# Layer normalisation bound by its transfers: hand-placed semaphores in one critical section, and the reciprocal moved to GpSimd as a power

## The chip, the core and the metric

The kernel runs on one core of one Trainium2 chip. The core has five engines that matter here: VectorE (DVE in the profile), ScalarE (ACT), GpSimd (POOL), SyncE (SP, which here only issues transfers) and 16 DMA engines that move data between the chip's main memory (HBM) and the core's working memory (SBUF). The metric is the device time of one execution in microseconds, the median of several. The profile's span runs from the first to the last instruction and is some 1.7 to 2.3 us shorter than the time.

## The reference, cut to what matters

```python
batch, seq, dim = 32, 512, 1024          # x: 64 MB of float32
def reference(x, eps):                   # eps = 1e-5
    mean = np.mean(x, axis=-1, keepdims=True)
    var = np.var(x, axis=-1, keepdims=True)
    return ((x - mean) / np.sqrt(var + eps)).astype(np.float32)
```

16,384 rows of 1,024 numbers are each normalised on their own. 67.1 MB have to be read and 67.1 MB written.

## The kernel before

SBUF holds a ring with places for 50 rows in each of 128 partitions. The work goes in 15 tiles of 2 to 10 rows per partition. A tile is loaded into its place, normalised there, and stored from there; then the place is free for a later tile. The framework (Tile) finds the dependencies and places the semaphores.

```python
TILES = (4, 6, 10, 10, 10, 10, 10, 10, 10, 10, 10, 10, 10, 6, 2)
RING = 50
GROUP = 10      # rows computed together
FINE = 6        # ... in the last LAST tiles
LAST = 3

def group(xs, G):
    # VectorE: two statistics per row: (count, mean, squared deviations) of each half of 512
    for k in range(G): ... nc.vector.bn_stats(out=stats[:, k, s, :], in_=xs[:, k, ...])
    # GpSimd: nine small operations that merge them into -mean (nmean) and the sum of squares (ss)
    ...
    nc.scalar.activation(out=std[:, :G], in_=ss[:, :G], func=AF.Sqrt, bias=eps_t, scale=1.0 / D)
    nc.vector.reciprocal(out=rstd[:, :G], in_=std[:, :G])
    nc.gpsimd.tensor_mul(out=nmr[:, :G], in0=nmean[:, :G], in1=rstd[:, :G])
    for k in range(G):     # ScalarE: x * rstd + nmr, in place
        nc.scalar.activation(out=xs[:, k, :], in_=xs[:, k, :], func=AF.Identity,
                             bias=nmr[:, k : k + 1], scale=rstd[:, k : k + 1])

with tc.manual_schedule():
    for t, (K, row, pos) in enumerate(plan):
        nc.sync.dma_start(out=ring[:, pos : pos + K, :], in_=rows_of(x2, row, K))      # load
        step = FINE if t >= len(TILES) - LAST else GROUP
        for g in range(0, K, step): ... group(...)
        nc.scalar.dma_start(out=rows_of(o2, row, K), in_=ring[:, pos : pos + K, :])    # store
```

I count tiles, loads and stores from 0: store 12 is the store of the last tile of 10 rows, third from the end.

## Time and profile before

| | before |
|---|---|
| time, median of the first 3 runs | 318.13 us (318.11 to 318.26) |
| span of the profiled run | 316.6 us |
| busy: VectorE, ScalarE, GpSimd | 49%, 48%, 12% |
| share of the DMA engines' time: loads, stores | 49.6%, 49.1% |
| mean rate | 424 GB/s |
| first load issued, its first packet | 0.72 us, 1.75 us |
| last packet ends, span ends | 315.2 us, 316.6 us |

The last two rows and some later numbers come from the trace's packet records, which give queue, size, start and duration of every packet that a DMA engine moved. The profile has no name for the engine of a packet, but each transfer is completed by all 16 of them one by one, and the time from the first to the last completion, called the *spread* below, says how far the engines have drifted apart.

Three lines of ScalarE's timeline (start, length, what; in brackets its idle time and what ended it) show the path of the first tile: the square root, four normalisations, and the issue of the first store.

```profile
16.10 0.30 ACT L95 ACTIVATE std<-ss,eps_t 128x4 f32<-128x4 f32 x1 [13.88 <-POOL ss L60]
16.92 4.63 ACT L103 ACTIVATE ring<-ring,nmr,rstd 128x1024 f32<-128x1024 f32 x4 [0.53 <-POOL nmr L101]
21.58 0.37 ACTq L127 DMA_DIRECT2D out_dram<-ring  x1
```

### The profile page before, as it was taken

To read this page: it belongs to the slowest core of one execution; us is meant where nothing else is said; L and a number is where in the kernel's file an instruction comes from. 1 tells how busy PE (TensorE), PEld (TensorE's weight loads), DVE (VectorE), ACT (ScalarE), POOL (GpSimd) and SP (SyncE) were. 2 spreads that over 40 slices of the span, in tenths; PEclk is the share of its full clock that TensorE was granted. 3 is DMA by queue.
4 is the path that set the end of the run, shared out by engine and by line. 5 is a ranking of instruction groups with operands and counts; after the bars stand their busy time and mean duration, and the time that the engine had idled before them with its cause. 6 is when DMAs were issued, how large, how long until landed. Compare 5 with 4: busy or idle time off the path is not lost.

```text
span 316.6 us, 712 instructions
## 1 busy us (share of the span) xinstructions
DVE 156.5 (49%) x273; ACT 152.6 (48%) x145; POOL 37.5 (12%) x164
## 2 busy tenths in 40 slices
DVE  0692939539139229229319309409509509654300
ACT  1065329294490391291292192193094094591730
POOL 0202030200300300300300300300300200222200
DMA  8999999999999999999999999999999999999995
GB/s 308 437 424 401 411 466 430 432 419 440 446 435 414 430 457 430 424 419 466 430 424 419 450 435 436 414 430 445 450 414 424 450 438 408 444 421 426 463 407 247
DMA packets 4324, 134.25 MB, mean 424 GB/s; under 512 B 480, under 2 KB 480, under 8 KB 480
## 3 DMA queue, kind: packets, MB, share of 16 engines
q1 hardware_dynamic: 2160, 67.11, 49.6%
q10 hardware_dynamic: 2160, 67.11, 49.1%
q14 instruction: 4, 0.03, 0.0%
HBM read 67.11 MB, written 67.11 MB: 424 GB/s over the span
## 4 chain that ended last, share of the span: by engine, by line
DMA 42%; DVE 26%; another core or an unknown queue 14%; POOL 6%; ACT 5%; issue 3%; SPq 0%; DVEq 0%; POOLq 0%
DMA ring<-in_x_dram 29%; DVE stats L68 26%; DMA out_dram<-ring 13%; ACT ring L103 4%; POOL half L57 1%; POOL dev L89 1%; ACT std L95 1%; POOL dev L92 1%; POOL dev L82 1%; POOL nmean L79 1%; POOL dev L88 1%; POOL nmean L60 1%; POOL ss L60 1%; DVE rstd L99 0%
## 5 line engine op out<-in xcount | busy, mean ns | idle before, releaser
L68 DVE BATCH_NORM_STATS2 stats<-ring 128x6 f32<-128x512 f32 x256 | 153.4, 677 | 92.5 <-DMA ring<-in_x_dram 92.5
L103 ACT ACTIVATE ring<-ring,nmr,rstd 128x1024 f32<-128x1024 f32 x128 | 146.5, 1226 | 8.9 <-POOL nmr L101 8.9
L95 ACT ACTIVATE std<-ss,eps_t 128x10 f32<-128x10 f32 (+3 forms) x16 | 4.8, 301 | 141.7 <-POOL ss L60 141.7
L57 POOL TENSOR_TENSOR half<-stats 128x20 f32<-128x20 f32 (+3 forms) x16 | 3.7, 233 | 243.2 <-DVE stats L68 243.2
L99 DVE RECIPROCAL rstd<-std 128x10 f32<-128x10 f32 (+3 forms) x16 | 3.3, 204 | 51.7 <-ACT std L95 51.7
L89 POOL TENSOR_SCALAR dev<-dev 128x40 f32<-128x40 f32 (+3 forms) x16 | 4.6, 289 | 1.4
L101 POOL TENSOR_TENSOR nmr<-nmean,rstd 128x10 f32<-128x10 f32 (+3 forms) x16 | 3.3, 205 | 10.4 <-DVE rstd L99 10.4
L92 POOL TENSOR_TENSOR dev<-dev,stats 128x40 f32<-128x40 f32 (+3 forms) x16 | 4.1, 259 | 1.3
L79 POOL TENSOR_SCALAR nmean<-nmean 128x10 f32<-128x10 f32 (+3 forms) x16 | 3.9, 244 | 1.4
L82 POOL TENSOR_TENSOR dev<-stats,nmean 128x40 f32<-128x40 f32 (+3 forms) x16 | 3.9, 245 | 1.3
L88 POOL TENSOR_TENSOR dev<-dev 128x40 f32<-128x40 f32 (+3 forms) x16 | 3.8, 239 | 1.3
L57 POOL TENSOR_TENSOR half<-dev 128x20 f32<-128x20 f32 (+3 forms) x16 | 3.4, 212 | 1.3
L60 POOL TENSOR_TENSOR nmean<-half 128x10 f32<-128x10 f32 (+3 forms) x16 | 3.2, 203 | 1.3
L60 POOL TENSOR_TENSOR ss<-half 128x10 f32<-128x10 f32 (+3 forms) x16 | 3.2, 203 | 1.3
L95 ACT ACT_TABLE_LOAD x1 | 1.3, 1283 | 0.9 <-DVE eps_t L120 0.9
L120 DVE MEMSET eps_t<- 128x1 f32 x1 | 0.1, 59 | 0.8 <-PEq L144 0.8
L144 POOL MEMSET const-float32-0.0<- 128x1 f32 x1 | 0.1, 98 | 0.2 <-issue 0.2
L144 POOL MEMSET const-uint8-127<- 128x1 uint8 x1 | 0.1, 102 | 0.0
L144 POOL MEMSET const-bfloat16-1.0<- 128x1 bf16 x1 | 0.1, 101 | 0.0
L144 POOL MEMSET const-float32-1.0<- 128x1 f32 x1 | 0.1, 98 | 0.0
## 6 DMA issues: line engine op xcount, KB each, us to landing
ring<-in_x_dram SPq DMA_DIRECT2D x11, 5120.0 KB, 52.4
out_dram<-ring ACTq DMA_DIRECT2D x11, 5120.0 KB, 41.0
ring<-in_x_dram SPq DMA_DIRECT2D x2, 3072.0 KB, 30.7
out_dram<-ring ACTq DMA_DIRECT2D x2, 3072.0 KB, 22.0
ring<-in_x_dram SPq DMA_DIRECT2D x1, 2048.0 KB, 7.8
out_dram<-ring ACTq DMA_DIRECT2D x1, 2048.0 KB, 22.4
ring<-in_x_dram SPq DMA_DIRECT2D x1, 1024.0 KB, 61.0
out_dram<-ring ACTq DMA_DIRECT2D x1, 1024.0 KB, 11.4
```

The lines of the kernel that those rows point to most:

```text
L57: nc.gpsimd.tensor_tensor(out=half[:, :G], in0=terms[:, :, 0:2], in1=terms[:, :, 2:4], op=ALU.add)
L60: nc.gpsimd.tensor_tensor(out=o, in0=half[:, :G, 0], in1=half[:, :G, 1], op=ALU.add)
L68: nc.vector.bn_stats(out=stats[:, k, s, :], in_=xs[:, k, s * BN_MAX : (s + 1) * BN_MAX],)
L79: nc.gpsimd.tensor_scalar(out=nmean[:, :G], in0=nmean[:, :G], scalar1=-1.0 / H, scalar2=None, op0=ALU.mult)
L82: nc.gpsimd.tensor_tensor(out=dev[:, :G], in0=mean4, in1=nmean[:, :G].unsqueeze(2).to_broadcast([P, G, H]), op=ALU.add,)
L88: nc.gpsimd.tensor_mul(out=dev[:, :G], in0=dev[:, :G], in1=dev[:, :G])
L89: nc.gpsimd.tensor_scalar(out=dev[:, :G], in0=dev[:, :G], scalar1=float(D // H), scalar2=None, op0=ALU.mult)
L92: nc.gpsimd.tensor_tensor(out=dev[:, :G], in0=dev[:, :G], in1=m2, op=ALU.add)
L95: nc.scalar.activation(out=std[:, :G], in_=ss[:, :G], func=AF.Sqrt, bias=eps_t, scale=1.0 / D)
L99: nc.vector.reciprocal(out=rstd[:, :G], in_=std[:, :G])
L101: nc.gpsimd.tensor_mul(out=nmr[:, :G], in0=nmean[:, :G], in1=rstd[:, :G])
L103: nc.scalar.activation(out=xs[:, k, :], in_=xs[:, k, :], func=AF.Identity, bias=nmr[:, k : k + 1], scale=rstd[:, k : k + 1],)
```

## The change

The intent: free VectorE from waiting for its reciprocal (51.7 us of waits), let it run ahead through all statistics, and replace the framework's semaphores by few hand-placed ones.

```diff
-RING = 50
-GROUP = 10
-FINE = 6
-LAST = 3
+SLOT, SLOTS = 10, 5
...
+    ctx.enter_context(tc.tile_critical(no_gpsimd_drain=True))
...
+    stored = {p: sem(f"stored_{p[0]}_{p[1]}") for p in places}     # one count of stores per ring place
+    taken, pool, act = sem("taken"), sem("pool"), sem("act")
...
-        nc.vector.reciprocal(out=rstd[:, :G], in_=std[:, :G])
+        n = gp(
+            g.tensor_tensor(
+                out=rstd[:, b, :K], in0=std[:, b, :K], in1=power[:, :K], op=ALU.pow    # power = -1
+            ),
+            other=(act, row + t + 1),
+        )
...
+    for p in places:
+        n = sum(1 for q in plan if (q[2], q[0]) == p)
+        nc.sync.wait_ge(stored[p], 16 * n)
```

(Cut: the same GpSimd operations and normalisations as before, each with its wait and its increment written out.) One thing goes without a word of its own: with `FINE` and `LAST` the splitting of the last 10-row tile into 6 + 4 rows for computing is gone.

More of the change, by code (lines that the diff above doesn't have):

```diff
@@ L10 @@
 TILES = (4, 6, 10, 10, 10, 10, 10, 10, 10, 10, 10, 10, 10, 6, 2)
-RING = 50
-GROUP = 10
-FINE = 6
-LAST = 3
+SLOT, SLOTS = 10, 5
+FIRST, TURNS = 3, 2
 @with_exitstack
@@ L38 @@
     assert sum(TILES) * P == N
-    rings = ctx.enter_context(tc.tile_pool(name="rings", bufs=1))
-    st = ctx.enter_context(tc.tile_pool(name="st", bufs=3))
-    sm = ctx.enter_context(tc.tile_pool(name="sm", bufs=10))
     fdt = mybir.dt.float32
@@ L46, with sbuf @@
     ALU = mybir.AluOpType
-    ring = rings.tile([P, RING, D], fdt)
-    eps_t = rings.tile([P, 1], fdt)
+    def sbuf(name, shape):
+        return ctx.enter_context(nc.sbuf_tensor(name, shape, fdt))
+    plan, row, pos = [], 0, 0
+    for K in TILES:
+        at = pos % (SLOT * SLOTS)
+        plan.append((K, row, at, at // SLOT))
+        row += K
+        pos += K
+    ctx.enter_context(tc.tile_critical(no_gpsimd_drain=True))
+    ring = sbuf("ring", [P, SLOT * SLOTS, D])
+    stats = sbuf("stats", [P, SLOT * SLOTS, NSUB, 6])
@@ new lines @@
+    half = sbuf("half", [P, SLOT, 2])
+    dev = sbuf("dev", [P, SLOT, H])
+    ss, nmean, std, rstd, nmr = (
+        sbuf(n, [P, 2, SLOT]) for n in ("ss", "nmean", "std", "rstd", "nmr")
+    )
+    eps_t = sbuf("eps_t", [P, 1])
+    power = sbuf("power", [P, SLOT])
+    sem = nc.alloc_semaphore
+    places = sorted({(at, K) for K, row, at, slot in plan})
+    landed = [sem(f"landed_{t}") for t in range(FIRST + SLOTS)]
+    for t in range(len(landed), len(plan)):
+        looped = t < FIRST + TURNS * SLOTS
+        landed.append(landed[t - SLOTS] if looped else sem(f"landed_{t}"))
@@ L51, in rows_of @@
+    stored = {p: sem(f"stored_{p[0]}_{p[1]}") for p in places}
+    taken, pool, act = sem("taken"), sem("pool"), sem("act")
     def rows_of(a, row, K):
         return a[row * P : (row + K) * P].rearrange("(p k) d -> p k d", p=P)
-    def pool_sum(o, terms):
-        G = terms.shape[1]
-        half = sm.tile([P, GROUP, 2], fdt, name="half")
-        nc.gpsimd.tensor_tensor(
-            out=half[:, :G], in0=terms[:, :, 0:2], in1=terms[:, :, 2:4], op=ALU.add
-        )
-        nc.gpsimd.tensor_tensor(
-            out=o, in0=half[:, :G, 0], in1=half[:, :G, 1], op=ALU.add
-        )
@@ L64, in group @@
-    def group(xs, G):
-        stats = st.tile([P, GROUP, NSUB, 6], fdt, name="stats")
-        for k in range(G):
-            for s in range(NSUB):
-                nc.vector.bn_stats(
-                    out=stats[:, k, s, :],
-                    in_=xs[:, k, s * BN_MAX : (s + 1) * BN_MAX],
-                )
-        parts = stats[:, :G].rearrange("p g s (h c) -> p g (s h) c", h=2)
-        mean4, m2 = parts[:, :, :, 1], parts[:, :, :, 2]
-        nmean = sm.tile([P, GROUP], fdt, name="nmean")
-        dev = sm.tile([P, GROUP, H], fdt, name="dev")
-        ss = sm.tile([P, GROUP], fdt, name="ss")
-        pool_sum(nmean[:, :G], mean4)
-        nc.gpsimd.tensor_scalar(
-            out=nmean[:, :G], in0=nmean[:, :G], scalar1=-1.0 / H, scalar2=None, op0=ALU.mult
-        )
-        nc.gpsimd.tensor_tensor(
-            out=dev[:, :G],
-            in0=mean4,
-            in1=nmean[:, :G].unsqueeze(2).to_broadcast([P, G, H]),
-            op=ALU.add,
-        )
-        nc.gpsimd.tensor_mul(out=dev[:, :G], in0=dev[:, :G], in1=dev[:, :G])
-        nc.gpsimd.tensor_scalar(
-            out=dev[:, :G], in0=dev[:, :G], scalar1=float(D // H), scalar2=None, op0=ALU.mult
-        )
-        nc.gpsimd.tensor_tensor(out=dev[:, :G], in0=dev[:, :G], in1=m2, op=ALU.add)
-        pool_sum(ss[:, :G], dev[:, :G])
-        std = sm.tile([P, GROUP], fdt, name="std")
-        nc.scalar.activation(
-            out=std[:, :G], in_=ss[:, :G], func=AF.Sqrt, bias=eps_t, scale=1.0 / D
-        )
-        rstd = sm.tile([P, GROUP], fdt, name="rstd")
-        nc.vector.reciprocal(out=rstd[:, :G], in_=std[:, :G])
-        nmr = sm.tile([P, GROUP], fdt, name="nmr")
-        nc.gpsimd.tensor_mul(out=nmr[:, :G], in0=nmean[:, :G], in1=rstd[:, :G])
-        for k in range(G):
-            nc.scalar.activation(
-                out=xs[:, k, :],
-                in_=xs[:, k, :],
-                func=AF.Identity,
-                bias=nmr[:, k : k + 1],
-                scale=rstd[:, k : k + 1],
-            )
@@ L111 @@
-    plan, row, pos = [], 0, 0
-    for K in TILES:
-        if pos + K > RING:
-            pos = 0
-        plan.append((K, row, pos))
-        row += K
-        pos += K
-    with tc.manual_schedule():
-        nc.vector.memset(eps_t, eps_val)
-        for t, (K, row, pos) in enumerate(plan):
-            nc.sync.dma_start(out=ring[:, pos : pos + K, :], in_=rows_of(x2, row, K))
-            step = FINE if t >= len(TILES) - LAST else GROUP
-            for g in range(0, K, step):
-                G = min(step, K - g)
-                group(ring[:, pos + g : pos + g + G, :], G)
-            nc.scalar.dma_start(out=rows_of(o2, row, K), in_=ring[:, pos : pos + K, :])
+    owner, wait = {}, []
@@ new lines @@
+    count = {p: 0 for p in places}
+    for t, (K, row, at, slot) in enumerate(plan):
+        gone = sorted({owner[r] for r in range(at, at + K) if r in owner})
+        for g in gone:
+            p = plan[g][2], plan[g][0]
+            if g == gone[-1]:
+                break
+            nc.sync.wait_ge(stored[p], 16 * sum(1 for q in plan[: g + 1] if (q[2], q[0]) == p))
+        dma = nc.sync.dma_start(out=ring[:, at : at + K, :], in_=rows_of(x2, row, K))
+        if gone:
+            p = plan[gone[-1]][2], plan[gone[-1]][0]
+            n = sum(1 for q in plan[: gone[-1] + 1] if (q[2], q[0]) == p)
+            dma._wait_ge(stored[p], 16 * n)
+        dma.then_inc(landed[t], 16)
+        owner.update((r, t) for r in range(at, at + K))
@@ new lines, in statistics @@
+    def statistics(t, arrived):
+        K, row, at, slot = plan[t]
+        for k in range(K):
+            for s in range(NSUB):
+                i = nc.vector.bn_stats(
+                    out=stats[:, at + k, s, :],
+                    in_=ring[:, at + k, s * BN_MAX : (s + 1) * BN_MAX],
+                )
+                if k == 0 and s == 0:
+                    i._wait_ge(landed[t], arrived)
+                if k == K - 1 and s == NSUB - 1:
+                    i.then_inc(taken, 1)
+    nc.vector.memset(eps_t[:], eps_val)
@@ new lines, with gp @@
+    nc.vector.memset(power[:], -1.0)
+    for t in range(len(plan)):
+        turn = (t - FIRST) // SLOTS if FIRST <= t < FIRST + TURNS * SLOTS else 0
+        statistics(t, 16 * (turn + 1))
+    npool, after_std, ready = 0, [], []
+    def gp(i, own=None, other=None):
+        nonlocal npool
+        if other is not None:
+            i._wait_ge(*other)
+        elif own:
+            i._wait_ge(pool, own)
+        i.then_inc(pool, 1)
+        npool += 1
+        return npool
+    g = nc.gpsimd
@@ new lines @@
+    for t, (K, row, at, slot) in enumerate(plan):
+        b = t % 2
+        parts = stats[:, at : at + K].rearrange("p g s (h c) -> p g (s h) c", h=2)
+        mean4, m2 = parts[:, :, :, 1], parts[:, :, :, 2]
+        nm, d, h = nmean[:, b, :K], dev[:, :K], half[:, :K]
+        n = gp(
+            g.tensor_tensor(out=h, in0=mean4[:, :, 0:2], in1=mean4[:, :, 2:4], op=ALU.add),
+            other=(taken, t + 1),
+        )
+        n = gp(g.tensor_tensor(out=nm, in0=h[:, :, 0], in1=h[:, :, 1], op=ALU.add), n)
+        n = gp(
+            g.tensor_scalar(out=nm, in0=nm, scalar1=-1.0 / H, scalar2=None, op0=ALU.mult), n
+        )
+        n = gp(
+            g.tensor_tensor(
+                out=d, in0=mean4, in1=nm.unsqueeze(2).to_broadcast([P, K, H]), op=ALU.add
+            ),
+            n,
+        )
+        n = gp(g.tensor_mul(out=d, in0=d, in1=d), n)
+        n = gp(
+            g.tensor_scalar(
+                out=d, in0=d, scalar1=float(D // H), scalar2=None, op0=ALU.mult
+            ),
+            n,
+        )
+        n = gp(g.tensor_tensor(out=d, in0=d, in1=m2, op=ALU.add), n)
+        n = gp(g.tensor_tensor(out=h, in0=d[:, :, 0:2], in1=d[:, :, 2:4], op=ALU.add), n)
+        n = gp(
+            g.tensor_tensor(out=ss[:, b, :K], in0=h[:, :, 0], in1=h[:, :, 1], op=ALU.add), n
+        )
+        after_std.append(n)
+        n = gp(
+            g.tensor_tensor(
+                out=rstd[:, b, :K], in0=std[:, b, :K], in1=power[:, :K], op=ALU.pow
+            ),
+            other=(act, row + t + 1),
+        )
+        ready.append(
+            gp(g.tensor_mul(out=nmr[:, b, :K], in0=nm, in1=rstd[:, b, :K]), n)
+        )
@@ new lines @@
+    for t, (K, row, at, slot) in enumerate(plan):
+        b = t % 2
+        nc.scalar.activation(
+            out=std[:, b, :K],
+            in_=ss[:, b, :K],
+            func=AF.Sqrt,
+            bias=eps_t[:],
+            scale=1.0 / D,
+        )._wait_ge(pool, after_std[t]).then_inc(act, 1)
+        for k in range(K):
+            i = nc.scalar.activation(
+                out=ring[:, at + k, :],
+                in_=ring[:, at + k, :],
+                func=AF.Identity,
+                bias=nmr[:, b, k : k + 1],
+                scale=rstd[:, b, k : k + 1],
+            ).then_inc(act, 1)
+            if k == 0:
+                i._wait_ge(pool, ready[t])
+        nc.scalar.dma_start(
+            out=rows_of(o2, row, K), in_=ring[:, at : at + K, :]
+        )._wait_ge(act, row + K + t + 1).then_inc(stored[at, K], 16)
```

## The prediction

> **What bounds the kernel now.** I read the page's 40 slices first, then the DMA queues, then the stretches at both ends, then the waits, and only then the costs of single instructions.
>
> ```profile
> DVE  0692939539139229229319309409509509654300
> ACT  1065329294490391291292192193094094591730
> POOL 0202030200300300300300300300300200222200
> DMA  8999999999999999999999999999999999999995
> ...
> q1 hardware_dynamic: 2160, 67.11, 49.6%
> q10 hardware_dynamic: 2160, 67.11, 49.1%
> ```
>
> The reader is to see that no compute engine has a slice pattern near 9, while the 16 DMA engines have it from the first slice to the last. Loads (q1) and stores (q10) take 49.6 + 49.1 = 98.7% of all DMA time. The remaining 1.3% of 316.6 us is 4.1 us: everything that a change which moves no bytes away can hope for. The same in stretches of the span (start:end, length, busy us of DVE, ACT and POOL with counts, TensorE clock, DMA share, GB/s):
>
> ```profile
> 0.00:2.00 2.00, 0.06 (x1) 1.07 (x1) 0.19 (x4) 1.00 0.60 115
> 2.00:8.00 6.00, 0.00 (x0) 0.21 (x1) 0.00 (x0) 1.00 0.90 369
> ...
> 100.00:200.00 100.00, 52.03 (x91) 46.90 (x44) 9.71 (x40) 1.00 1.00 433
> ...
> 304.00:310.00 6.00, 0.00 (x0) 0.17 (x1) 0.00 (x0) 1.00 1.03 445
> 310.00:313.00 3.00, 0.00 (x0) 0.00 (x0) 0.00 (x0) 1.00 0.85 360
> 313.00:315.00 2.00, 0.00 (x0) 0.00 (x0) 0.00 (x0) 1.00 0.23 94
> 315.00:316.00 1.00, 0.00 (x0) 0.00 (x0) 0.00 (x0) 1.00 0.00 0
> ```
>
> The middle runs full at 433 GB/s. What is not full is the first load's issue and ramp, and the last five microseconds: 3 x 0.15 + 2 x 0.77 + 1.6 = 3.6 us, in which some of the 16 engines have finished and others still carry their last packets, and then the program ends.
>
> The largest waits look like opportunities and are not:
>
> ```profile
> ACT std L95 <- POOL ss L60: 141.7, 16, 13.9
> DVE stats L68 <- DMA ring<-in_x_dram: 92.5, 14, 8.8
> DVE rstd L99 <- ACT std L95: 51.7, 16, 3.3
> ```
>
> The third is the one the change removes: VectorE stands 16 times some 3.2 us in front of its reciprocal, because the chain VectorE, GpSimd, ScalarE, VectorE is a round trip. But the second shows VectorE idle another 92.5 us for want of loaded data. In the steady state the 3.2 us only shorten that wait.
>
> **What the Trainium skill says.** "DMA: Bandwidth & Descriptors", section Specifications, gives a fabric ceiling of 435 GB/s for a core's 16 DMA engines. The trace agrees: 433 GB/s between 100 and 200 us, and 436 between 200 and 280. The same page, section "Queues, rings and completion order", says that each DMA engine goes round-robin between the queues that have work, a packet at a time. The trace agrees in an instructive place: the last load is 1 MB in packets of 8 KB, the stores beside it have packets of 40 KB, and this load lands 14.6 us after its predecessor (295.3 against 280.7 us in the packet records). If packets alternate it must wait for (8 + 40)/8 = 6 times its own bytes: 6.3 MB at 430 GB/s, 14.6 us. So while either queue has work, the engines stay full, whichever queue it is.
> "GPSIMD Engine Reference", section 3.1, puts GpSimd elementwise work about 2 times slower than VectorE at 2048 elements; this trace has only tiny operands, where they hardly differ (multiply of 128x10 on GpSimd 208 ns, reciprocal on VectorE 204 ns). I found no page with the cost of a power on GpSimd.
>
> **The change, part by part.**
> (a) Bytes, transfer sizes, ring places and issuing queues are unchanged: 15 loads on SyncE's queue, 15 stores on ScalarE's. 134.2 MB at 433 GB/s, an estimate from the steady stretch, is 310 us in both kernels.
> (b) Load gating. Before, load 6 (counting from 0) issues at 64.16 us, load 7 at 88.33, load 8 at 112.56; the packet records have stores 1, 2 and 3 complete at 63.63, 87.81 and 112.00. Each load leaves some 0.5 us after the store that frees its place. The hand-placed counts wait for the very same stores (load 6 for stores 0 and 1, load 7 for store 2, and so on; loads 13 and 14 both for store 8). The only false wait that goes is load 5: it waited until 8.55 us for load 0's semaphore. Behind it the queue already held loads 1 to 4, which land as late as 67.75 us. Gain: 0.
> (c) Reciprocal to GpSimd. 16 reciprocals (3.3 us busy in all) leave VectorE; 15 powers come to GpSimd, which is 12% busy. If one costs 0.3 to 1 us, 5 to 15 us more of POOL's time; of the chain of a tile, the 0.2 us reciprocal and a 0.08 us hop go and the power comes. The path that this lies on ends in a store's issue, so I compare each store's issue with when its queue gets to it (packet records, completion of the store before it):
> store 1: issued 34.3, wanted about 41.5; store 3: 75.0, wanted 85.1; store 5: 119.8, wanted 133.4; store 11: 264.9, wanted 274.9; store 12: 285.3, wanted 290.7; store 13: 299.0, wanted 303.4; store 14: 304.2, wanted 310.6.
> Every store waits at least 4 us in its queue. A power of up to some 3 us changes nothing at the end.
> (d) The 10-row tile third from the end is no longer cut in 6 + 4. It lands at 261.4. Its 20 statistics take 11.98 us (to 273.4), nine small GpSimd operations 2.95 (276.3), square root, power and multiply about 1.0 (277.3), ten normalisations 11.42: store 12 leaves at 288.7 rather than 285.3, 3.4 us later. It is wanted at 290.7 by the fastest engine, and a first packet follows an issue by about 1 us (load 0: issued 0.72, first packet 1.75). 289.7 is still in time, by 1 us, and the last load is on the queues until 293.4. Cost: 0. The last two tiles land when they did before (281, 295), when VectorE and ScalarE are free again, so the stores 13 and 14 keep their times.
> (e) The start. SyncE gets a no-operation, a semaphore round and a further branch ahead of its first load, as do the others for theirs. The first issue now comes at 0.72 us, after a start of which the semaphore round is about 0.65. Chosen: +0.2 us.
> (f) The end. After the last packet (315.25 us) come 1.3 us to the end of the span. After the change SyncE passes nine waits, of which two come after the one that matters (places sorted, the last store's is seventh), then gathers all engines and releases them, ahead of the same final barrier. With hops of 0.05 to 0.08 us as between operations here: +0.2 us.
> Sum: 0 + 0.2 + 0.2 = +0.4 us, on 318.13: 318.5 us.
>
> **The rivals.**
> 1. The chain does matter, and freeing VectorE of 51.7 us of waiting pays. For it: the chain of waits that ended last gives statistics 26% of the span. Against it: that chain follows the loads, which are themselves held back by stores sharing the engines; DMA is full throughout. It could gain no more than what DMA leaves idle, 4.1 us, and really only at the ends: 314.5 us at the very best. The early stores do leave sooner (store 1 by about 3 us), but into a queue that already has work, and with reads alone just as fast (449 GB/s from 8 to 21 us) nothing is gained by it.
> 2. The power on GpSimd is slow software, several us a tile. For it: no row of this trace prices it. Against: it needs over 3 us a tile to open a gap in the store queue. At 5 us the last store would leave at about 309 instead of 304.2, 1.6 us short of its turn at 310.6; perhaps +1 us: 319.5.
> 3. Store 12, 3.4 us later, opens a gap after all: fast engines are out of work between 290.7 and its first packet. At worst 1 to 2 us on the fast engines; the slow ones, which set the end, finish store 11 only at 293.1. Under +0.5 us.
> 4. The program's own ends move more than I think: the hand-made exit avoids a GpSimd drain (a gain of some tenths), or the entry has to fetch instructions after its jump (a loss of 1 or 2 us).
>
> **Range and chances.** The mechanism says equal; the spread is that of (e), (f) and rivals 2 and 4, about 1 us each way: 317.4 to 319.7. Faster by 2% means 311.8 us, below what a full DMA of 310 us with the measured start (1.75 us to the first packet) and an end of 1.3 us allows: chance 0.01. Slower by 2% means 324.5 us: 6 us of new DMA idleness, only by a power of over 10 us or by a gate that I misread: 0.02.
>
> **What would show it.** In the changed kernel's profile: DMA still 9 in all slices but the ends, both queues near 98.5% together; SyncE's loads at the same times within 1 us (first +0.2, load 5 at about 3 us); VectorE's wait for ScalarE gone and its wait for loads larger by about as much; a row for the power under 1 us each; store 12 issued near 288.7, stores 13 and 14 near 299 and 304; 1.5 us from the last packet to the end. It would be wrong if slices below 9 appear in the middle (a gate or the power), if the first load leaves over 1 us later, or if the last packets end clearly before 315 us.

## The result, and the profile after

| | before | after |
|---|---|---|
| time, median | 318.19 us (318.11 to 318.63, 4 runs) | 319.74 us (318.77 to 320.15, 4 runs) |
| spans of the runs | 316.6 in the profiled one | 317.0, 317.8, 318.1, 318.4 |
| first load issued | 0.72 us | 0.93 us |
| store 0 / store 12 issued | 21.58 / 285.32 us | 22.66 / 292.72 us |
| last packet to end of span | 1.3 us | 1.7 us |

The ratio is 1.0041, 95% interval 1.0017 to 1.0066: the same within 2%, and slower by a little. (Ratios are the mean time of one kernel's fast runs over that of the other's of the same rounds, so not quite the ratio of the medians quoted.)

The waits that the change was to move, after (columns as in the prediction; VectorE's wait for its reciprocal is gone):

```profile
DVE stats L100 <- DMA ring<-in_x_dram: 143.1, 15, 12.8
ACT ring L185 <- POOL nmr L171: 32.3, 15, 2.4
```

The slices of the span for the DMA engines, after:

```profile
DMA  8999999999999999999999999999999999997995
GB/s 294 447 412 423 399 441 436 432 418 479 422 417 412 480 422 417 427 463 422 417 437 453 422 417 449 448 417 412 468 432 417 422 448 425 420 472 320 418 439 252
```

The reader is to see the single 7 before the end, with 320 GB/s: the only hole within the span. The stretches around it, first in the kernel before, then after (columns as in the prediction):

```profile
280.00:290.00 10.00, 7.39 (x13) 4.77 (x5) 1.32 (x6) 1.00 0.98 423
290.00:294.00 4.00, 0.19 (x1) 2.21 (x3) 1.11 (x5) 1.00 0.99 424
294.00:300.00 6.00, 2.47 (x4) 4.98 (x5) 1.15 (x6) 1.00 1.01 437
```

```profile
280.00:290.00 10.00, 6.81 (x12) 8.73 (x8) 1.16 (x2) 1.00 1.07 460
290.00:294.00 4.00, 0.40 (x1) 2.99 (x4) 2.45 (x10) 1.00 0.65 272
294.00:300.00 6.00, 2.47 (x4) 4.73 (x5) 2.85 (x10) 1.00 1.02 440
```

Between 290 and 294 us the DMA engines work 65% of the time, and by the packet records 1.58 us per engine are lost there. (The share above 1 in the stretch before it can only come from how packets are booked to stretches; by the records no engine is idle there.) What ScalarE did in that time, after the change, with the row of the power from the table of costliest groups:

```profile
278.58 0.30 ACT L177 ACTIVATE std<-ss,eps_t 128x10 f32<-128x10 f32 x1 [10.08 <-POOL ss L159]
281.27 11.42 ACT L185 ACTIVATE ring<-ring,nmr,rstd 128x1024 f32<-128x1024 f32 x10 [2.38 <-POOL nmr L171]
292.72 0.34 ACTq L194 DMA_DIRECT2D out_dram<-ring  x1
...
L165 POOL TENSOR_TENSOR rstd<-std,power 128x10 f32<-128x10 f32 (+3 forms) x15 | 26.3, 1753 | 8.5 <-ACT std L177 8.5
```

The normalisations stand 2.38 us idle for the power and the multiply after it. One power takes 1.04 us for 4 rows, 1.35 for 6 and 1.98 for 10. Store 12 leaves at 292.72 us, while store 11 is complete from 291.3 us (its first engine) to 294.2 (its last): several engines have nothing to store, and the small last load is soon used up.

The difference of the two profiled spans, 1.82 us, adds up from the packet records: first packet 0.18 later; hole 1.58; more time in the packets themselves, 312.61 against 312.26 us per engine, 0.36; last packet to the end 0.44 more; and 0.7 us back, because the engines finish closer together. So far theory A: the late store. But this is the slowest of four runs, and a hole cannot tell why the other runs, at 317.0 to 318.1 us, differ among themselves.

### The profile page after: what moved, and what is told of

Read it like the earlier page. It is cut to its first block, busy times and chain, and to the rows that moved or that the text cites. A ratio compares the mean times of both kernels' runs of the same rounds, so it can differ in the third digit from the quotient of the medians.

```text
span 318.4 us, 659 instructions
## 1 busy us (share of the span) xinstructions
DVE 153.5 (48%) x258; ACT 152.2 (48%) x144; POOL 62.2 (20%) x169
## 4 chain that ended last, share of the span: by engine, by line
DMA 42%; DVE 25%; another core or an unknown queue 18%; ACT 7%; POOL 3%; issue 1%; SPq 0%; ACTq 0%
DMA ring<-in_x_dram 30%; DVE stats L100 25%; DMA out_dram<-ring 12%; ACT ring L185 7%; POOL rstd L165 1%; SPq L87 0%; ACT std L177 0%; POOL nmr L171 0%; POOL dev L151 0%; POOL dev L156 0%; POOL nmean L141 0%; POOL dev L144 0%; POOL dev L149 0%; POOL half L136 0%
## 5 line engine op out<-in xcount | busy, mean ns | idle before, releaser
L100 DVE BATCH_NORM_STATS2 stats<-ring 128x6 f32<-128x512 f32 x256 | 153.4, 677 | 143.1 <-DMA ring<-in_x_dram 143.1
L165 POOL TENSOR_TENSOR rstd<-std,power 128x10 f32<-128x10 f32 (+3 forms) x15 | 26.3, 1753 | 8.5 <-ACT std L177 8.5
## 6 DMA issues: line engine op xcount, KB each, us to landing
out_dram<-ring ACTq DMA_DIRECT2D x1, 2048.0 KB, 21.5
```

The lines of the kernel that those rows point to most:

```text
L100: i = nc.vector.bn_stats(out=stats[:, at + k, s, :], in_=ring[:, at + k, s * BN_MAX : (s + 1) * BN_MAX],)
L165: g.tensor_tensor(out=rstd[:, b, :K], in0=std[:, b, :K], in1=power[:, :K], op=ALU.pow),
```

## The experiments

Twelve kernels were run, all correct, each against runs of the kernel before in the same rounds. The diffs show the deciding lines; the allocations and semaphore counts that follow from them are cut. Names: those with *a* are built on the changed kernel, those with *b* on the kernel before.

### Taking the parts away: a_split, a_recip, a_split_recip; adding them: b_pow_whole

**a_split** computes tile 12 as 6 + 4 rows again, with one store:

```diff
-    for t, (K, row, at, slot) in enumerate(plan):
+    for gi, (t, k0, K) in enumerate(groups):      # tile 12 is in groups as 6 + 4 rows
```

> The changed kernel with the 10-row tile third from the end computed as 6 + 4 rows again (one store as ever). Theory A, the late store: in the changed kernel this tile's store left at 292.7 us, after the store queue had run dry (engines short of work for 1.6 us between 290 and 294), because the tile is computed whole (+3.4 us) and its power takes 2.0 us. Here the store should leave near 289, the DMA hole should vanish and 0.6 to 1.6 us of the time with it: 318.7 us, ratio to before 1.001 to 1.003. Theory B, the ends: all that the change costs is in the entry and exit of the critical section and in the luck of how far the DMA engines drift apart: unchanged, 319.5, ratio 1.004.

**a_recip** puts the reciprocal back on VectorE, after the tile's statistics:

```diff
+        nc.vector.reciprocal(
+            out=rstd[:, t % 2, :K], in_=std[:, t % 2, :K]
+        )._wait_ge(act, row + t + 1).then_inc(inverse, 1)
```

> The changed kernel with the reciprocal on VectorE again in place of the power on GpSimd; semaphores by hand, last 10-row tile whole. Theory A: the store third from the end leaves some 1.8 us earlier, near 291, when the store queue has just run dry on the fastest engines only: hole of 0 to 0.4 us, 318.9 us, ratio 1.001 to 1.003. Theory B: 319.5, ratio 1.004. VectorE waits for ScalarE again, 48 us in all, which costs nothing by either theory.

**a_split_recip** does both, so that only the critical section and its semaphores remain of the change:

> The changed kernel with both undone: reciprocal on VectorE and the tile third from the end as 6 + 4; what stays is the critical section and its semaphores. Theory A: no hole, and what remains against before is entry and exit, 0.15 + 0.45 us as the profile of the changed kernel shows them: 318.7 us, ratio 1.002. Theory B: the same as the changed kernel, 1.004. If the semaphores cost nothing it is 1.000.

**b_pow_whole** is the kernel before with the two arithmetic parts alone (`LAST = 2`, and the power in place of the reciprocal):

> The kernel before with the two arithmetic parts of the change alone: power on GpSimd, and the tile third from the end computed whole; semaphores as before. Theory A: its store leaves at about 290.5 to 292, depending on when the slowest DMA engine delivers the load, a hole of 0.1 to 1 us: 318.3 to 319.0 us, ratio 1.001 to 1.003. Theory B: as before, ratio 1.000.

| | time | ratio (95%) | spans of the runs | store 12 issued |
|---|---|---|---|---|
| a_split | 319.67 | 1.0045 (1.0032 to 1.0057) | 316.9, 317.7, 317.4, 316.9, 317.9 | 286.6 |
| a_recip | 318.79 | 1.0018 (1.0004 to 1.0031) | 317.3, 317.0, 317.0, 317.1, 316.8 | 290.6 |
| a_split_recip | 318.59 | 1.0014 (1.0001 to 1.0026) | 316.8, 316.8, 316.8, 316.8, 316.9 | 286.2 |
| b_pow_whole | 318.11 | 1.0005 (0.9993 to 1.0018) | 316.3, 316.2, 317.4, 316.8, 316.2 | 290.4 |

Theory A, as the whole cause, falls on a_split: store 12 is in time there and the profile has no hole, yet the time is that of the changed kernel, and the runs still differ by 1.0 us. A part of the loss for the hole is not excluded: 2.2 us of a_split's time lie outside the span, in the other *a* kernels 1.7 to 2.1, and by the spans alone a_split is some 0.5 us shorter than the changed kernel (means 317.4 and 317.8 us), which runs that differ by 1 us cannot settle. What the table shows besides: kernels with the reciprocal have runs within 0.5 us of each other and those with the power do not, whatever the semaphores. (In later rounds the kernel before had single runs of 318.78 and 318.98 us, 0.55 and 0.74 above the medians of their rounds, so the sign is weaker than these runs make it look.) And a_split_recip isolates the cost of the critical section: 0.4 us, and it is steady. Its first packet comes at 1.93 us against 1.75, and 1.8 us pass from its last packet to the end, against 1.3.

(Why more of a_split's time lies outside the span stays open.)

### Is it the power? b_pow, b_whole, a_split_pow2; and b_warm

**b_pow** is the kernel before with the power alone:

```diff
-        nc.vector.reciprocal(out=rstd[:, :G], in_=std[:, :G])
+        nc.gpsimd.tensor_tensor(
+            out=rstd[:, :G], in0=std[:, :G], in1=power[:, :G], op=ALU.pow
+        )
```

> The kernel before with the power on GpSimd as the only change. Its store third from the end should leave by about 287, before its queue is empty, so theory A, the late store, says: as before, 318.2 us, ratio 1.000, and no spread. Theory D, formed on the last runs: every kernel with the power has runs that differ by a microsecond (spans 316.2 to 317.4 in the kernel before with power and whole tile, 316.9 to 317.9 in the changed kernel with the tile split) and no kernel with the reciprocal has (316.1 to 316.3; 316.8 to 316.9), so the power itself disturbs something: then spans from 316.2 to 317.3 and a ratio of 1.001 to 1.003.

**b_whole** has the whole tile 12 alone:

```diff
-LAST = 3
+LAST = 2
```

> The kernel before with the tile third from the end computed whole as the only change. Its store should leave near 288.7. Theory A: in time, 318.2 us, ratio 1.000. If a store at 288.7 is already late on the fastest engines, up to 0.2 us more, ratio 1.0005. Theory D: as before and without spread.

**a_split_pow2** is a_split with each power done twice in a row:

> The changed kernel with the tile third from the end as 6 + 4 rows, and every power done twice: a dose of the power without a late store (it should leave near 289 at the latest). Theory A: as with one power, the added 26 us on GpSimd are hidden: 319.5 us. Theory D, the power disturbs: the spread grows, spans from 317 to 319, median ratio 1.006 or more.

**b_warm** is an attempt to beat both kernels by a tiny early write:

```diff
+        nc.vector.memset(first, 0.0)
+        nc.scalar.dma_start(out=o2[N - P : N, 0:128], in_=first)
```

> An attempt to beat both: in every profile the load packets in flight when the first store begins, near 24 to 26 us, take about 0.7 us longer once on each of the 16 engines (11 to 13 us of engine time, 0.7 us of the span). If that is a cost of the first write on each engine, a tiny early write (64 KB, overwritten later by the right result) while the first load is still in its latency takes it in the shadow: 317.6 us, ratio 0.998. If it is a cost of beginning to mix large reads and writes, it stays: 318.2 us, ratio 1.000.

| | time | ratio (95%) | spans of the runs |
|---|---|---|---|
| b_pow | 318.93 | 1.0018 (1.0006 to 1.0030) | 316.9, 316.3, 316.9, 317.0, 316.1 |
| b_whole | 318.04 | 0.9998 (0.9985 to 1.0011) | 316.1, 316.2, 316.3, 316.2 |
| a_split_pow2 | 342.18 | 1.0730 (1.0691 to 1.0770) | 336.5 to 346.9 |
| b_warm | 318.18 | 1.0004 (0.9990 to 1.0019) | 316.2, 316.3, 316.3, 316.3 |

b_warm is a miss: 19 load packets around the time when the stores begin still take some 0.5 us longer. (The 11 to 13 us of engine time expected "in every profile" are 7 to 13 us by the packet records before 30 us.) b_whole costs nothing. The power alone gives the spread of 0.9 us in the kernel before too. And the second power costs not 0 us, nor 1, but 22 us beyond a_split. No theory that I had written down expected that. The profile of a_split_pow2:

```profile
DVE  0765858192192094067049029119207607744200
ACT  1056239391840840570390192094085048175830
POOL 0343161606106103301500700600510240634310
DMA  7999999999999999999999999999999995955993
```

No compute engine is near its limit (GpSimd is 27% busy), and the DMA engines are "full" until late, but they do the same work more slowly. In the packet records a store packet of 40 KB, which takes 1.51 us in the other kernels so far (but for one packet of the changed kernel), takes over 10% longer 288 times out of 1,408; from 69 us on it is about four packets in every round of packets, that is, about four engines (four of the 16 completions of load 12 come 22 us or more after the first).

### The work of the power, or its delay? a_offpath_pow2 and a_delay

**a_offpath_pow2** is a_split_recip with two powers per group that nobody waits for, after the multiply that ScalarE waits for:

```diff
+        for _ in range(2):
+            n = gp(
+                g.tensor_tensor(
+                    out=junk[:, :K], in0=std[:, b, :K], in1=power[:, :K], op=ALU.pow
+                ),
+                npool,
+            )
```

> What in two powers a group made 342 us of 319.7? Here the hand-placed kernel with the reciprocal on VectorE (318.6 us alone) also does two powers a group on GpSimd, but after the work that ScalarE waits for, into a scrap tile: the work of the powers without their delay. Theory D, powers on GpSimd disturb the transfers: about 340 us again, store packets of some engines some 0.3 us longer. Theory E, the delay shifts the stores against the loads and the DMA engines then get in each other's way: no delay, so 318.6 us and no spread.

**a_delay** is its counterpart, with short multiplications in place of the powers, in the way:

```diff
+        for d in range({10: 13, 6: 9, 4: 7, 2: 5}[K]):
+            n = gp(
+                g.tensor_mul(out=junk[:, :K], in0=nm, in1=power[:, :K]),
+                n,
+                (inverse, gi + 1) if d == 0 else None,
+            )
```

> The counterpart: the hand-placed kernel with the reciprocal on VectorE and 5 to 13 short multiplications into a scrap tile on GpSimd, in the way of ScalarE, which take as long as two powers (3.7 us for a 10-row tile): the delay without a power. Theory E: 335 to 345 us, with store packets that take longer, spread over the 16 engines growing to 20 us or more. Theory D: 318.6 to 319 us and a spread of 1 to 3 us.

a_offpath_pow2: 318.58 us (spans 316.7 to 316.9), ratio 1.0008 (0.9993 to 1.0023). a_delay: 348.41 us (spans 346.5 to 347.2), ratio 1.0943 (1.0925 to 1.0961). The DMA row of a_offpath_pow2, and its row of the scrap powers:

```profile
DMA  8999999999999999999999999999999999999995
...
L185 POOL TENSOR_TENSOR junk<-std,power 128x10 f32<-128x10 f32 (+3 forms) x32 | 52.9, 1652 | 2.5
```

52.9 us of powers beside the transfers disturb nothing measurable. In a_delay 36.0 us of multiplications, with the gaps between them, stand in the way: the normalisations of a 10-row tile begin 3.7 us later (their idle time before is 4.27 us against 0.57 in a_split_recip), and that costs 30 us. Theory D is dead, theory E stands: it is the delay. But by the reckoning of the prediction a delay of 4 us is hidden by store queues with 4 to 14 us in hand. So where does it do harm?

### Where is the delay harmful? a_delay_early and a_delay_first

**a_delay_early** delays the first three tiles only:

```diff
-        for d in range({10: 13, 6: 9, 4: 7, 2: 5}[K]):
+        for d in range({10: 13, 6: 9, 4: 7, 2: 5}[K] if gi < 3 else 0):
```

> Where does the delay do its harm? As the kernel with the delay (348.4 us), but only the first three tiles (4, 6 and 10 rows) are delayed, the other twelve not. In that kernel's packet records 3 of the 16 DMA engines fall out of step with the rest from the third store on (from 69 us their store packets take 0.3 to 0.8 us longer) and never come back. Theory F, the step is lost at the start, where a late first or third store finds its DMA engines in different places: 335 to 350 us again, though nothing is delayed after 60 us. Theory G, it is the later normalisations that come too late, tile after tile: 318.6 us.

346.84 us median (334.86 to 349.08). Three of the four runs are slow, being over 1.5% above the fastest of the kernel, and no ratio is given; the one fast run, 334.86 us, against the median of before of 318.23, suffices: with twelve tiles undelayed, 16 us at the least. This speaks for theory F.

**a_delay_first** delays the first tile alone (`if gi == 0`):

> Which of the three early tiles? Only the first (4 rows) is delayed, by 1.9 us; all others are as in the hand-placed kernel with the reciprocal on VectorE (318.6 us). Theory H, the first store: when it comes a DMA engine's packet later (first packets near 27.6 us on most of the 16 engines, not near 25.7), the engines begin to alternate reads and writes out of step, as the spread of the third load's completions shows (1.6 to 1.8 us in all kernels with spread or slowness, 0.6 to 1.0 us in the steady ones but the one with spread that was profiled in a good run): 330 to 350 us, or at the least runs that differ by over 1 us. Theory I, the third store, which in the delayed kernels was issued only 2.1 to 2.4 us before its first engine was free for it, against 3.6 to 4.0 in the steady ones: 318.6 us and no spread, as this one is on time here.

336.23 us median (333.57 to 347.76), ratio of the fast runs 1.0534 (1.0501 to 1.0567). The profile is of a fast run. The first tile on ScalarE, in a_split_recip and then in a_delay_first, which differ by nothing but seven small multiplications:

```profile
16.21 0.30 ACT L186 ACTIVATE std<-ss,eps_t 128x4 f32<-128x4 f32 x1 [14.04 <-POOL ss L170]
17.03 4.63 ACT L194 ACTIVATE ring<-ring,nmr,rstd 128x1024 f32<-128x1024 f32 x4 [0.53 <-POOL nmr L177]
21.69 0.38 ACTq L207 DMA_DIRECT2D out_dram<-ring  x1
```

```profile
16.13 0.30 ACT L195 ACTIVATE std<-ss,eps_t 128x4 f32<-128x4 f32 x1 [13.96 <-POOL ss L172]
18.89 4.63 ACT L203 ACTIVATE ring<-ring,nmr,rstd 128x1024 f32<-128x1024 f32 x4 [2.46 <-POOL nmr L185]
23.56 0.37 ACTq L216 DMA_DIRECT2D out_dram<-ring  x1
```

And what becomes of it 270 us later, in a_split_recip and in a_delay_first:

```profile
290.00:294.00 4.00, 0.19 (x1) 1.31 (x2) 1.81 (x8) 1.00 0.99 426
294.00:300.00 6.00, 2.47 (x4) 5.89 (x6) 0.61 (x3) 1.00 1.01 438
```

```profile
290.00:294.00 4.00, 2.01 (x4) 4.00 (x4) 1.41 (x7) 1.00 0.32 137
294.00:300.00 6.00, 4.05 (x8) 5.25 (x6) 0.74 (x4) 1.00 0.15 63
```

A share of 0.15 is two or three engines out of 16 still at work: the ones that fell behind. The others have done all that was issued, and each further load and store waits for the stragglers, because a transfer is complete only when all 16 engines have finished their parts. In the packet records 122 store packets of this run are slow (none in a_split_recip), 37.6 us too long in total. The completions show two late engines: from load 6 on, two of the 16 come apart from the rest, 3 us behind the next at load 6 and 15 us at load 12. Shared by two, the 37.6 us make each some 18 us late, which agrees with the spread of load 12, 17.5 us, and with the loss of time, 17.6 us.

Put together, all profiled kernels, roughly in the order of their first store's issue:

| kernel | store 0 issued, us | engines of 16 that begin it before 27 us | spread of load 2, us | spread of load 12, us | slow 40 KB store packets | time, us |
|---|---|---|---|---|---|---|
| b_whole | 21.5 | 15 | 0.8 | 2.9 | 0 | 318.0 |
| before | 21.6 | 14 | 1.0 | 1.9 | 0 | 318.2 |
| a_split_recip | 21.7 | 16 | 0.6 | 1.8 | 0 | 318.6 |
| b_warm | 21.7 | 16 | 0.7 | 1.8 | 0 | 318.2 |
| a_recip | 21.7 | 16 | 0.6 | 2.4 | 0 | 318.8 |
| a_offpath_pow2 | 21.7 | 16 | 0.6 | 1.9 | 0 | 318.6 |
| b_pow_whole | 22.3 | 0 | 0.8 | 2.0 | 0 | 318.1, 1.2 between runs |
| b_pow | 22.4 | 2 | 1.6 | 4.1 | 0 | 318.9, 0.9 between runs |
| a_split | 22.6 | 0 | 0.7 | 1.9 | 0 | 319.7, 1.0 between runs |
| after | 22.7 | 1 | 1.8 | 4.1 | 1 | 319.7, 1.4 between runs |
| a_split_pow2 | 23.5 | 0 | 1.8 | 25.9 | 288 | 342.2 |
| a_delay_early (slow run) | 23.5 | 0 | 1.8 | 30.3 | 195 | 346.8 |
| a_delay_first | 23.6 | 0 | 1.9 | 17.5 | 122 | 336.2 |
| a_delay | 23.7 | 0 | 1.8 | 31.0 | 188 | 348.4 |

(Slow is over 10% longer than the usual 1.514 us. Load 2, the first one of 10 rows, is in flight when the stores begin. Where engines lag by more than a load, completions of two loads mix in time; there the spread is taken from the semaphore of load 12 alone.) In the four slow profiles the spread of load 12, 17.5 to 31.0 us, is within 2 us of what the profiled run took beyond a_split_recip's 318.6 us: 17.3, 24.1, 28.3 and 30.4. The time is lost to the engines that fall behind.

A packet of 40 KB takes 1.5 us. If store 0 is issued by 21.7 us, nearly all engines begin it between two packets of load 2 near 25.7 us. If it is issued 0.6 us later they have already begun the next load packet, and the first store packet comes near 27.7. The step is in the third column, and it lies between the steady kernels and the others. From 22.3 to 22.7 us it is a lottery: some runs are as good as before, some 1 us slower, and the two profiles of good runs (b_pow_whole, a_split) have a small spread of load 2, the two of poorer runs a large one. At 23.5 us and later every run measured was 15 us slower or more.

The third column does not tell the lottery from the certain loss, though: issued at 22.3 or at 23.6 us, store 0 begins on nearly all engines between 27.5 and 28.4 us. One difference is in the completions of load 2. In each of the four slow profiles one or two of the 16 come at 27.3 to 27.5 us, 0.9 to 1.2 us ahead of the rest, and in no other profile; the large spread of load 2 in *after* and b_pow is made by one or two that come late. In a_delay_first two come early and two engines fall behind, but in a_split_pow2, a_delay_early and a_delay it is one and four, one and three, two and three. So this is a trace to follow and not an explanation.

What remains open: why a late first store makes two to four engines write more slowly for some 200 us (in a_delay_first the slow packets begin between 71.6 and 271.6 us). That the engines alternate between loads and stores packet by packet is in the records; the trace names no engine and no place in memory, and no run here shows a mechanism. Also not separated: whether 1 us of the first store's delay is enough for the lottery by itself (a kernel with the power on the first tile alone was not run).

## Why the prediction was right or wrong

- **What bounds the kernel** was right, in the plain sense: the transfers, in both kernels. The compute waits changed as foretold: VectorE's wait for ScalarE is gone, its wait for loads grew from 92.5 to 143.1 us, and nothing was gained by it.
- **(a), (b)** right: the loads that wait for a store are issued within 0.1 us of where they were, from 64.17 us (before 64.16) to 234.34 us (before 234.39); load 5 no longer waits.
- **(c)** is the step that failed. Its size: a power was put at "0.3 to 1 us" and takes 1.98 us for 10 rows. Its reasoning: "A power of up to some 3 us changes nothing at the end" looked only at stores that queue behind another store. The first store queues behind nothing, and I left it out of the list. Rival 1 even had it in hand, "with reads alone just as fast nothing is gained by it", and took for granted that a store's place among the reads cannot matter. It does: in a_delay_first a first store issued 1.9 us later costs 15 us or more. What the 1.1 us by which store 0 is late in the changed kernel cost there was not measured alone.
- **(d)** right that the whole tile by itself costs nothing, wrong in its margin. Store 12 was to leave at 288.7 us, 1 us before it was needed, and left at 292.7 in the profiled run: 1.8 us more by the power, 2.2 us more because the slowest DMA engine delivered the tile late and its statistics began at 263.6 us rather than 261.4. Where the engines keep together the whole tile costs nothing (b_whole 0.9998) or, with the later start of the hand-placed kernel, 0.2 us (a_recip against a_split_recip, within the noise).
- **(e)** +0.2 us: measured +0.18 to the first packet. **(f)** +0.2 us: measured +0.44.
- **The sum**: +0.4 us was foretold, +1.55 came between the medians. By the runs: ends 0.4 (a_split_recip), whole tile 0.2 (a_recip, within the noise); the remaining 0.95 came with the power. That it came through the first store's lateness is the likely reading and not a shown one: in the profiled run the late store 12 had a part, and in the kernel before the power cost less (ratio 1.0018 in b_pow, 1.0005 in b_pow_whole). The mechanism, the same time within 2%, held, and the power is the mis-sized term: 1.98 us for 10 rows. The median, 319.74 us, lies 0.04 us above the range of 317.4 to 319.7. It came as near as that because the range allowed for a slow power and for moving ends, not because the sum was right.
- **What would show it**: of the signs that were named, the power under 1 us, store 12 near 288.7 us and stores 13 and 14 near 299 and 304 us (they left at 302.2 and 306.4) did not come. One sign of being wrong did: a slice below 9 within the span, from the power and the late load together.
- **One misread line**: 449 GB/s with reads alone, from 8 to 21 us, comes of how packets are booked to stretches (the DMA share in that line is 1.04). Packets cut at the edges of the stretch give 433 GB/s, as between 100 and 200 us, so the conclusion stands.
- **Rival 2** came nearest (a slow power, 319.5 us), for a reason that was not the real one.

No version beats the kernel before beyond the noise; b_whole equals it.

## What to carry to other kernels

When a kernel is bound by its DMA engines, "the queue has work" does not prove that a delay is hidden: look at the transfers that have nothing queued ahead of them, above all the first one in the other direction. Where two transfer streams share the engines, compare the spread of a transfer's completions over the 16 engines between two versions; when it grows from tile to tile, some engines are falling behind and every transfer waits for them. And when runs of one kernel begin to differ by more than those of its parent, treat that as a finding, and enlarge the suspect until the effect is plain: doubling a 2 us operation turned a 1 us doubt into 22 us.

## What the Trainium skill lacked or had wrong

- No page gives the cost of a power on GpSimd. In these runs it takes 1.04 us for 4, 1.35 us for 6 and 1.98 us for 10 float32 values per partition (128 partitions), over nine times a multiply of 10 values (0.21 us). "GPSIMD Engine Reference", section 3.1, has only the sum.
- "DMA: Bandwidth & Descriptors", section "Queues, rings and completion order", describes the round-robin of an engine between its queues, and the records agree with it; it does not say that the moment at which a second stream joins can set the rate for the rest of the run. Here, the same transfers with the first store 1.9 us later: 336.2 us against 318.6, with 122 of 1,408 store packets slow against none.
- The same page gives about 0.6 us for the first byte on the queues used here (section Specifications). The first load agrees: its issue takes from 0.72 to 1.09 us, and its first packet starts at 1.75 us, 0.66 us later. The page has no figure for a transfer that comes behind packets of another queue: the first packets of store 0 start 3.7 to 4.6 us after its issue on fourteen engines (21.58 us to between 25.3 and 26.2), and on the other two only at about 28 us.
- No page mentions that the load packets in flight when the first stores begin take longer: in every profile 14 to 25 of those before 30 us, by 0.4 to 0.7 us on the mean, and an early small write does not take it away (b_warm, 19 packets by 0.5 us).
